# Gated DeltaNet layer on one core: both halves of a group through the block inversion together

## The chip, the cores and the metric

The kernel runs on one core of a Trainium2 chip (eight cores, of which seven stay idle). The metric is the device time of one execution in microseconds. The kernel before was timed three times; the profile is of a fourth execution.

## The reference

One layer of a decoder trunk: adaptive RMSNorm of x (1,024 tokens, width 1,024), a gated DeltaNet mixer, a gated residual and a final RMSNorm. The mixer projects to q and k (8 heads of 128), v and a gate z (16 heads of 128) and two rows of gates, runs a causal convolution of 4 taps with SiLU over q, k and v, and then works in chunks. Cut to what matters:

```python
a_mat = where(strict, einsum('bhncd,bhnsd->bhncs', kb, k) * decay, 0.0)
t_mat = triangular_solve(a_mat + eye, eye, lower=True, unit_diagonal=True)   # an inverse for each chunk and head
u = t_mat @ (v * beta); w = t_mat @ (kb * exp(gc))
def step(state, inp):                    # a scan over the chunks
    v_new = uc - wc @ state
    o = qd @ state + qkc @ v_new
    state = state * gl + kd.T @ v_new
o = rms_norm(o) * silu(z); y = o @ w_out
```

The part that the change touches is `t_mat`, the inverse of a unit lower triangular matrix for each chunk and head.

## The kernel before, in words

The kernel takes chunks of 128 tokens, so a head has 8 chunks, and works on 8 groups of two value heads that share one q and k head. Each group has 16 triangular matrices of 128×128, in two halves (`hf`) of four chunks times two heads. A group passes through these stages.

- `proj_kq` and `values` project the group's q, k and v with three matmuls of 128×512 for each of 8 blocks of width (L448; 24 of them fill one PSUM bank of tag `pj`). Each result goes through `Conv` (ScalarE copies and scales it, L431 and L433, VectorE adds three taps, L435, ScalarE applies SiLU, L436). `turn` in `values` transposes a value tile on TensorE (L628) into a bank of `trans()`, 40 projection matmuls after that tile was done, and VectorE empties the bank (L629).
- `stage_a` makes the matrices `at` and sends their diagonal 32×32 blocks through HBM (D1) to a layout in which VectorE inverts all of them at once by forward substitution (L564 and L566). The result goes to HBM (D2). Then the stage waits D_L0.
- `levels(gi, G, hf)` builds the inverse of one half from the 32×32 inverses, in four steps. Eight DMAs for the group (L585, four a half) fetch the blocks into `TT`; VectorE transposes them into `TE` (L586 to L588). Step 1 multiplies `at` blocks with `TE` (L592 and L594, 16 matmuls of 32×32 in two corners of the array, written to `pa`); ScalarE and VectorE negate the result into `pn` (L598 and L599). Step 2 multiplies `pn` with `TT` (L602 and L603, `px`); VectorE copies the result to `TT` twice and transposes it to `TE` (L606 to L608). Step 3 multiplies 64×64 blocks (L611, `pb`) and ScalarE negates (L614). Step 4 (L617, `pc`) ends with a copy into `TT` (L618). Each of `pa`, `px`, `pb` and `pc` takes a fresh bank from `trans()`: tag `tr`, two banks, shared with L628 and with the transposes of `norms` (L497, L504), the products of `stage_a` (L538) and the matmul of the residual gate (L782).
- `scan` runs the recurrence over the 8 chunks of the group; `TT` of the first half is needed from its first chunk on (L744).

The order of TensorE's instructions is written out by hand: everything runs inside a `manual_schedule` for that engine, and `drive` plays the stages as generators against a model clock. A stage yields a cost (model ns on TensorE) and a delay; it isn't asked again until the delay has passed. While no stage is due, `drive` emits filler, that is projection matmuls, each counted as MM = 216. For group `gi`, one call of `drive` runs `scan(gi)`, `stage_a(gi + 1)` with its levels, and `values(gi + 1)` and `proj_kq(gi + 2)` as filler. For the two groups in `LEV1` (0 and 7) the second half's levels run in the next call, beside the group's own scan. When the stages of a call are done, the filler that is left follows. The order on the other engines, the queue of DMAs on SyncE (SP) among them, is not written out: the Tile framework chooses it and adds the semaphores.

The delays before: D_L1, D_L2 and D_L3 are 1,600, 1,800 and 1,600. The steps of one half, cut to their skeleton:

```python
pa = v8(trans())          # step 1: 16 matmuls, L592 and L594
yield 400, D_L1
px = v8(trans())          # step 2: 16 matmuls, L602 and L603, behind pn (L598, L599)
yield 670, D_L2
pb = v8(trans())          # step 3: 8 matmuls of 64x64, L611, behind L606, L607, L608
yield 430, D_L3
pc = v8(trans())          # step 4: 8 matmuls of 64x64, L617, behind pn2 (L614)
yield 430, D_L3
```

Of the kernel before, what the change touches and what calls it, by code (L numbers as in the profile page):

```python
# [9 lines left out]
F32 = mybir.dt.float32  # L10
# [7 lines left out]
P = 128  # L18
# [12 lines left out]
LEV1 = (0, 7)  # L31
# [6 lines left out]
START, START1 = 8000, 65000  # L38
D_G, D_RG = 6000, 11000
D_N, D_A0, D_A = 3000, 1500, 1000  # L40
D_L0, D_L1, D_L2, D_L3 = 46000, 1600, 1800, 1600
D_R, D_V, D_S = 500, 1100, 700
D_F0, D_F = 8000, 2000

# [2 lines left out]
def gdn_layer(ctx: ExitStack, tc: tile.TileContext, x, c, ada_w, ada_b, norm_g, w_in, conv_w, a_log, dt_bias,  # L47
# [8 lines left out]
    nc = tc.nc  # L56
# [12 lines left out]
    x, c, ada_w, ada_b, norm_g = x[0], c, ada_w[0], ada_b, norm_g  # L69
# [342 lines left out]
    cp = ctx.enter_context(tc.tile_pool(name="cp", bufs=2))  # L412
    TTs = [cp.tile([P, 4, 2, P], F32, name=f"TT{i}", bufs=1) for i in range(3)]
    for t in TTs:
        nc.gpsimd.memset(t, 0.0)
    TE = cp.tile([96, 8, 64], F32, name="TE", bufs=1)
    nc.gpsimd.memset(TE[0:64], 0.0)

    class Conv:

# [32 lines left out]
    def trans():  # L453
        return bank("tr", (P, 4, P))
# [68 lines left out]
    def stage_a(gi, G):  # L523

        kq, ats = G.kq, []
        if not hasattr(G, "bkd"):
            yield from norms(gi, G)
        D1 = dram.tile([16, P, 32], F32, name="D1", tag="D1", bufs=2)
        D2 = dram.tile([16, 4, 16, 2, 32], F32, name="D2", tag="D2", bufs=2)
        yield 0, D_A0  # L530
        for hf in range(NHALF):
            em, brk = G.em[hf], G.brk[hf]

            at = cp.tile([P, 8, P], F32, name="at", tag="at", bufs=2)
            for j in range(4):
                js = slice(j * P, (j + 1) * P)
                pg2 = trans()
                nc.tensor.matmul(pg2[:, 0:2], lhsT=kq[hf][:, 0, js], rhs=kq[hf][:, :, js], start=True, stop=True)  # L538
                for h in range(2):
                    nc.vector.scalar_tensor_tensor(at[:, 2 * j + h], pg2[:, 0], brk[:, j, h:h + 1], em[:, h, j],  # L540
                                                   op0=ALU.mult, op1=ALU.mult)
                nc.vector.tensor_tensor(em[:, :, j], em[:, :, j], pg2[:, 1:2].to_broadcast([P, 2, P]), op=ALU.mult)
                yield 430, D_A
            us = slice(8 * hf, 8 * hf + 8)
            for b in range(4):
                bs = slice(32 * b, 32 * b + 32)
                nc.sync.dma_start(out=D1[us, bs, :].rearrange("u s c -> s u c"), in_=at[bs, :, bs])
            ats.append(at)


        ua = cp.tile([P, 32, 32], F32, name="ua", tag="ua", bufs=1)
        for p in range(2):
            nc.sync.dma_start(out=ua[64 * p:64 * p + 64].rearrange("p s c -> p (s c)"),
                              in_=D1.rearrange("u (b s) c -> (u b) (s c)", b=4))
        tb = cp.tile([P, 16, 32], F32, name="tb", tag="tb", bufs=1)
        tm = cp.tile([P, 136], F32, name="tm", tag="tm", bufs=1)
        tbf = tb.rearrange("p m i -> p (m i)")
        nc.gpsimd.memset(tb, 0.0)
        nc.gpsimd.memset(tbf[0:64, 0:512:34], 1.0)
        nc.gpsimd.memset(tbf[64:128, 1:512:34], 1.0)  # L560
        for j in range(31):
            mm, ln = j // 2 + 1, 31 - j
            tmv = tm[:, :mm * ln].rearrange("p (m l) -> p m l", l=ln)
            nc.vector.tensor_tensor(tmv, tb[:, :mm, j:j + 1].to_broadcast([P, mm, ln]),  # L564
                                    ua[:, j:j + 1, j + 1:].to_broadcast([P, mm, ln]), op=ALU.mult)
            nc.vector.tensor_tensor(tb[:, :mm, j + 1:], tb[:, :mm, j + 1:], tmv, op=ALU.subtract)  # L566
        for p in range(2):
            nc.sync.dma_start(out=D2[:, :, :, p, :].rearrange("u b m i -> (u b) m i"), in_=tb[64 * p:64 * p + 64])

        yield 0, D_L0  # L570
        G.ats, G.D2 = ats, D2
        yield from levels(gi, G, 0)
        if gi not in LEV1:
            yield from levels(gi, G, 1)

    def levels(gi, G, hf):

        TT = TTs[(2 * gi + hf) % 3]
        G.TT.append(TT)
        at = G.ats[hf]  # L580
        tt = TT.rearrange("p n h c -> p (n h) c")
        us = slice(8 * hf, 8 * hf + 8)
        for b in range(4):
            bs = slice(32 * b, 32 * b + 32)
            nc.sync.dma_start(out=tt[bs, :, bs], in_=G.D2[us, b].rearrange("u m p i -> (m p) u i"))  # L585
        nc.vector.transpose(TE[0:32, :, 0:32], tt[0:32, :, 0:32])  # L586
        nc.vector.transpose(TE[32:64, :, 32:64], tt[32:64, :, 32:64])
        nc.vector.transpose(TE[64:96, :, 0:32], tt[64:96, :, 64:96])  # L588
        v8 = lambda t: t.rearrange("p a (b c) -> p (a b) c", c=64)
        pa = v8(trans())  # L590
        for u in range(8):
            nc.tensor.matmul(pa[32:64, u, :32], lhsT=at[0:32, u, 32:64], rhs=TE[0:32, u, 0:32], start=True,  # L592
                             stop=True)
            nc.tensor.matmul(pa[96:128, u, :32], lhsT=at[64:96, u, 96:128], rhs=TE[64:96, u, 0:32], start=True,  # L594
                             stop=True, tile_position=(64, 96))
        yield 400, D_L1
        pn = cp.tile([P, 8, 32], F32, name="pn", tag="pn2", bufs=1)
        nc.scalar.mul(pn[32:64], pa[32:64, :, :32], -1.0)  # L598
        nc.vector.tensor_scalar_mul(pn[96:128], pa[96:128, :, :32], -1.0)  # L599
        px = v8(trans())  # L600
        for u in range(8):
            nc.tensor.matmul(px[0:32, u, :32], lhsT=pn[32:64, u], rhs=tt[32:64, u, 32:64], start=True, stop=True)  # L602
            nc.tensor.matmul(px[64:96, u, :32], lhsT=pn[96:128, u], rhs=tt[96:128, u, 96:128], start=True,  # L603
                             stop=True, tile_position=(96, 64))
        yield 670, D_L2
        nc.vector.tensor_copy(tt[0:32, :, 32:64], px[0:32, :, :32])  # L606
        nc.vector.tensor_copy(tt[64:96, :, 96:128], px[64:96, :, :32])  # L607
        nc.vector.transpose(TE[32:64, :, 0:32], px[0:32, :, :32])  # L608
        pb = v8(trans())
        for u in range(8):  # L610
            nc.tensor.matmul(pb[64:128, u], lhsT=at[0:64, u, 64:128], rhs=TE[0:64, u], start=True, stop=True)  # L611
        yield 430, D_L3
        pn2 = cp.tile([P, 8, 64], F32, name="pn2", tag="pn2", bufs=1)
        nc.scalar.mul(pn2[64:128], pb[64:128], -1.0)  # L614
        pc = v8(trans())
        for u in range(8):
            nc.tensor.matmul(pc[0:64, u], lhsT=pn2[64:128, u], rhs=tt[64:128, u, 64:128], start=True, stop=True)  # L617
        nc.vector.tensor_copy(tt[0:64, :, 64:128], pc[0:64])  # L618
        yield 430, D_L3

    def values(gi, G, more):

# [294 lines left out]
    with tc.manual_schedule(engines={nc.tensor.engine}):  # L917
# [6 lines left out]
        for gi in range(-1, HQ):  # L924
            running.append(gi)
            streams, filler = [], []
            gates = itertools.chain(*zgates[:ZQ[gi + 1]])
            del zgates[:ZQ[gi + 1]]
            if gi >= 0:
                if gi in LEV1:  # L930
                    streams.append(levels(gi, Gs[gi], 1))
                streams.append(scan(gi, Gs[gi]))
            if gi + 1 < HQ:
                if gi < 0:
                    streams.append(gate_steps)
                streams.append(stage_a(gi + 1, Gs[gi + 1]))
                if gi < 0:
                    streams.append(norms(1, Gs[1]))
                more = []
                if gi + 2 < HQ:  # L940
                    Gs[gi + 2].kq = []
                    more = proj_kq(gi + 2, Gs[gi + 2].kq)
                if gi + 2 == HQ:
                    more = itertools.islice(tail, NE)
                v = lambda m: values(gi + 1, Gs[gi + 1], m)
                filler += (more, v(gates)) if gi < 0 else (gates, v(more))
            else:
                filler.append(gates)
            if gi == RG:
                streams.append(residual_gate())  # L950
            drive(streams, filler, start=(D_G, START, START1) if gi < 0 else None, tail=tail if gi >= HQ - 2 else None)
# [8 lines left out]
    for tg in range(2):  # L960
# [7 lines left out]
                    out_product(acc[t][hf], t, gw, ww[hf], kt == EARLY, False)  # L968
        if wlast is None:
            wos += [[cp.tile([P, TH], F32R, name=n, tag=t, bufs=b)  # L970
                        for n, t, b in (("wohi", "sz", 2), ("wolo", ("pn2", "tb")[hf], 1))] for hf in range(1)]
            wlast = [[load_wo(kt, hf, wos[2 * i + hf]) for hf in range(2)] for i, kt in enumerate(last)]
        glast = [load_g(kt, tg, gos[i]) for i, kt in enumerate(last)]

# [50 lines left out]
```

## Time and profile before

| what | value |
|---|---|
| median of 3 runs | 1140.28 us (1137.90 to 1142.37) |
| the profiled execution's own time | 1136.89 us |
| its span, first to last instruction | 1135.2 us |
| busy time of PE, VectorE (DVE), ScalarE (ACT), GpSimd (POOL) | 1054.0, 764.9, 534.5, 454.0 us |
| mean granted TensorE clock | 0.969 |
| DMA | 119.46 MB, mean 105 GB/s |

Times in the profile are counted from the first instruction. PE is TensorE's matmul row. Its matmuls overlap and their ends are modelled, so what one costs in a stream is read from the distance of two starts. An "idle before" in brackets names what the engine waited for. [...]

### The profile page before, as it was taken

How to read it: one execution, taken by the hardware profiler on the slowest of the kernel's cores; microseconds unless marked ns; L12 is line 12 of the kernel's file. 1: busy time of each engine (PE TensorE's matmuls, PEld its weight loads, DVE VectorE, ACT ScalarE, POOL GpSimd, SP SyncE). 2: the span in 40 equal slices, each digit the busy share in tenths (PEclk: the TensorE clock that was granted, in tenths of full speed). 3: DMA queues.
4: the chain of work that ended last, by engine and by line, in shares of the span. 5: the costliest groups of instructions: out<-in, count | busy, mean ns of one | idle time of the engine just before them, and what ended most of it. 6: DMA issues, size and time to landing. Idle time of an engine off the chain costs nothing.

```text
span 1135.2 us, 18160 instructions
## 1 busy us (share of the span) xinstructions
PE 1054.0 (93%) x6195; PEld 847.9 (75%) x6195; DVE 764.9 (67%) x1937; ACT 534.5 (47%) x1414; POOL 454.0 (40%) x535
## 2 busy tenths in 40 slices
PE   7677999989999899989999999999999979999997
PEld 6455787767778678867876887788778858878785
DVE  5968794785579866965687578667756866614515
ACT  5556534444553445345543644364446423634523
POOL 4361213532253225323532353245215433954743
PEclk8888999999999899999999999999999989999999
DMA  9903314342135323421442153115313472346442
GB/s 281 238 19 123 75 57 117 84 126 61 29 100 179 96 54 80 144 56 29 112 121 66 29 149 93 39 45 160 75 29 88 155 222 76 121 144 187 157 121 74
DMA packets 188130, 119.46 MB, mean 105 GB/s; under 512 B 59733, under 2 KB 166534, under 8 KB 187014
## 3 DMA queue, kind: packets, MB, share of 16 engines
q1 hardware_dynamic: 187536, 118.20, 37.0%
q8 instruction: 49, 0.80, 0.3%
q14 instruction: 43, 0.35, 0.1%
q10 hardware_dynamic: 502, 0.10, 0.0%
HBM read 93.03 MB, written 25.24 MB: 104 GB/s over the span
## 4 chain that ended last, share of the span: by engine, by line
PE 37%; DVE 19%; issue 6%; POOL 6%; ACT 5%; DMA 5%; SPq 0%; POOLq 0%; DVEq 0%; ACTq 0%
PE pj L448 16%; DVE tb L566 4%; DVE tm L564 4%; PE pj L826 4%; DVE vT L435 3%; DVE em L486 3%; POOL wolo L123 2%; PE tr L538 2%; PE ks L725 2%; PE ks L756 2%; PE ts L744 1%; PE oq L698 1%; PE oq L751 1%; PE tr L611 1%; PE tr L617 1%
## 5 line engine op out<-in xcount | busy, mean ns | idle before, releaser
L123 POOL TENSOR_TENSOR wlo<-wraw,whi 128x512 fp32r<-128x512 f32 x92 | 124.8, 1365 | 140.6 <-ACT whi L122 106.3
L435 DVE SCALAR_TENSOR_TENSOR vT<-xb,taps,vT 128x512 f32<-128x512 f32 x96 | 84.6, 881 | 25.3 <-ACT vT L433 24.3
L435 DVE SCALAR_TENSOR_TENSOR kq<-xb,taps,kq 128x512 f32<-128x512 f32 x96 | 78.2, 823 | 11.9 <-ACT kq L433 10.0
L122 ACT CAST whi<-wraw 128x512 fp32r<-128x512 f32 x92 | 55.4, 618 | 62.3 <-PE pj L448 58.7
L687 POOL TENSOR_TENSOR oT<-oT,z 128x256 f32<-128x256 f32 x64 | 51.3, 801 | 82.2 <-ACT oT L686 74.9
L564 DVE TENSOR_TENSOR tm<-tb,ua 128x126 f32<-128x126 f32 (+22 forms) x248 | 79.1, 319 | 6.5 <-DMA ua<-D 1.6
L686 ACT ACTIVATE oT<-pot,cols 128x256 f32<-128x256 f32 x64 | 30.4, 474 | 110.4 <-PE pot L684 53.8
L448 PE MATMUL pj<-h1hia,whi 128*128 128x512 f32 x184 | 76.0, 413 | 6.7 <-ACT vT L433 6.7
L566 DVE TENSOR_TENSOR tb<-tb,tm 128x126 f32<-128x126 f32 (+22 forms) x248 | 77.3, 312 | 5.0 <-DVE tm L564 0.2
L448 PE MATMUL pj<-h1lob,whi 128*128 128x512 f32 x184 | 78.8, 428 | 0.0
L448 PE MATMUL pj<-h1hia,wlo 128*128 128x512 f32 x184 | 78.5, 427 | 0.0
L448 PE MATMUL pj<-h1hib,whi 128*128 128x512 f32 x184 | 78.3, 426 | 0.0
L448 PE MATMUL pj<-h0hia,whi 128*128 128x512 f32 x184 | 76.5, 416 | 1.3 <-ACT kq L433 1.3
L448 PE MATMUL pj<-h0lob,whi 128*128 128x512 f32 x184 | 77.7, 422 | 0.0
L448 PE MATMUL pj<-h1hib,wlo 128*128 128x512 f32 x184 | 77.1, 419 | 0.0
L448 PE MATMUL pj<-h1loa,whi 128*128 128x512 f32 x184 | 76.3, 415 | 0.0
L448 PE MATMUL pj<-h0hib,wlo 128*128 128x512 f32 x184 | 76.1, 413 | 0.0
L448 PE MATMUL pj<-h0loa,whi 128*128 128x512 f32 x184 | 75.7, 411 | 0.0
L448 PE MATMUL pj<-h0hia,wlo 128*128 128x512 f32 x184 | 75.5, 410 | 0.0
L428 POOL MEMSET xb<- 128x3 f32 x32 | 3.4, 109 | 179.8 <-DVE kq L435 90.8
L448 PE MATMUL pj<-h0hib,whi 128*128 128x512 f32 x184 | 74.8, 407 | 0.0
L708 POOL TENSOR_TENSOR sso<-sso,neg_half 128x2 f32<-128x2 f32 x64 | 44.6, 697 | 58.4 <-DVE sso L707 57.7
(445 smaller groups left out, 2938.0 us busy)
## 6 DMA issues: line engine op xcount, KB each, us to landing
wraw<-in_gdn_w_in SPq DMA_DIRECT2D x92, 256.0 KB, 2.9
woraw<-in_gdn_w_out SPq DMA_DIRECT2D x54, 256.0 KB, 3.1
wa<-in_ada_w SPq DMA_DIRECT2D x16, 512.0 KB, 6.4
em<-gc_dram SPq DMA_DIRECT2D x8, 1024.0 KB, 5.2
z_dram<-sz SPq DMA_DIRECT2D x32, 256.0 KB, 2.5
z<-z_dram SPq DMA_DIRECT2D x64, 128.0 KB, 2.4
o_dram<-oT SPq DMA_DIRECT2D x64, 128.0 KB, 1.9
gsrc<-o_dram SPq DMA_DIRECT2D x32, 256.0 KB, 3.0
```

The lines of the kernel that those rows point to most:

```text
L122: nc.scalar.copy(hi, raw)
L123: nc.gpsimd.tensor_tensor(lo, raw, hi.bitcast(F32), op=ALU.subtract)
L435: nc.vector.scalar_tensor_tensor(dst, xb[:, j:j + TH], tp[:, j], dst, op0=ALU.mult, op1=ALU.add)
L448: nc.tensor.matmul(ps[:m], lhsT=a[:, k, :m], rhs=b[half][k // 4][:, k % 4], start=(k == 0 and n == 0), stop=(k == KT - 1 and n == 2))
L486: nc.vector.scalar_tensor_tensor(em[:, h, n], em[:, h, n], ngc[:, n, h0 + h:h0 + h + 1], mask, op0=ALU.add, op1=ALU.add)
L538: nc.tensor.matmul(pg2[:, 0:2], lhsT=kq[hf][:, 0, js], rhs=kq[hf][:, :, js], start=True, stop=True)
L564: nc.vector.tensor_tensor(tmv, tb[:, :mm, j:j + 1].to_broadcast([P, mm, ln]), ua[:, j:j + 1, j + 1:].to_broadcast([P, mm, ln]), op=ALU.mult)
L566: nc.vector.tensor_tensor(tb[:, :mm, j + 1:], tb[:, :mm, j + 1:], tmv, op=ALU.subtract)
L686: nc.scalar.mul(oT, pot, normw_c)
L687: nc.gpsimd.tensor_tensor(oT, oT, zs.pop(n), op=ALU.mult)
L708: nc.gpsimd.tensor_tensor(sso, sso, neg_half[:, :2], op=ALU.pow)
L826: nc.tensor.matmul(acc, lhsT=a[:, ts], rhs=b, start=(first and n == 0), stop=(last and n == 2))
```

## The change

`levels` takes a tuple of halves. Groups 1 to 6 call it once with both halves, groups 0 and 7 with one half at a time as before. Within a call each step is done for all its halves before the next yield, with a bank of `trans()` for each half; `TE` gets a second copy and `pn2` a second buffer. The transposes behind step 2 move ahead of the copies. D_L1, D_L2 and D_L3 become 2,600, 2,800 and 2,000, and step 2's model cost for a half 400 instead of 670. The DMA scratch (`dynamic_dma_scratch_size`) is set to 1,024, and the tile of the last stage that reuses tag `pn2` follows its two buffers.

```diff
-D_L0, D_L1, D_L2, D_L3 = 46000, 1600, 1800, 1600
+D_L0, D_L1, D_L2, D_L3 = 46000, 2600, 2800, 2000
...
-    TE = cp.tile([96, 8, 64], F32, name="TE", bufs=1)
-    nc.gpsimd.memset(TE[0:64], 0.0)
+    TEs = [cp.tile([96, 8, 64], F32, name=f"TE{i}", bufs=1) for i in range(2)]
+    for t in TEs:
+        nc.gpsimd.memset(t[0:64], 0.0)
...
-        yield from levels(gi, G, 0)
-        if gi not in LEV1:
-            yield from levels(gi, G, 1)
+        yield from levels(gi, G, (0,) if gi in LEV1 else (0, 1))
...
+        for i, hf in enumerate(hfs):
+            us = slice(8 * hf, 8 * hf + 8)
+            for b in range(4):
+                bs = slice(32 * b, 32 * b + 32)
+                nc.sync.dma_start(out=tt[i][bs, :, bs], in_=G.D2[us, b].rearrange("u m p i -> (m p) u i"))
+            nc.vector.transpose(TE[i][0:32, :, 0:32], tt[i][0:32, :, 0:32])
...
+        pa = [v8(trans()) for _ in every]
+        for i in every:
+            for u in range(8):
+                nc.tensor.matmul(pa[i][32:64, u, :32], lhsT=at[i][0:32, u, 32:64], rhs=TE[i][0:32, u, 0:32], start=True,
+                                 stop=True)
...
+        yield 400 * len(hfs), D_L1
+        pn = [cp.tile([P, 8, 32], F32, name="pn", tag="pn2", bufs=2) for _ in every]
+        for i in every:
+            nc.scalar.mul(pn[i][32:64], pa[i][32:64, :, :32], -1.0)
+            nc.vector.tensor_scalar_mul(pn[i][96:128], pa[i][96:128, :, :32], -1.0)
+        px = [v8(trans()) for _ in every]
...
+        yield 400 * len(hfs), D_L2
+        for i in every:
+            nc.vector.transpose(TE[i][32:64, :, 0:32], px[i][0:32, :, :32])
+        for i in every:
+            nc.vector.tensor_copy(tt[i][0:32, :, 32:64], px[i][0:32, :, :32])
+            nc.vector.tensor_copy(tt[i][64:96, :, 96:128], px[i][64:96, :, :32])
+        pb = [v8(trans()) for _ in every]
...
+        yield 430 * len(hfs), D_L3
+        pn2 = [cp.tile([P, 8, 64], F32, name="pn2", tag="pn2", bufs=2) for _ in every]
+        for i in every:
+            nc.scalar.mul(pn2[i][64:128], pb[i][64:128], -1.0)
+        pc = [v8(trans()) for _ in every]
...
+        yield 430 * len(hfs), D_L3
...
-    nc = bacc.Bacc("TRN2", target_bir_lowering=False, num_devices=1)
+    nc = bacc.Bacc("TRN2", target_bir_lowering=False, num_devices=1, dynamic_dma_scratch_size=1024)
```

## Rows read from the trace of the kernel before

**Rows 1.** Page, busy us (share of the span) and instructions of each engine.

```profile
PE 1054.0 (93%) x6195; PEld 847.9 (75%) x6195; DVE 764.9 (67%) x1937; ACT 534.5 (47%) x1414; POOL 454.0 (40%) x535
```

**Rows 2.** Page, the chain that ended last, share of the span by line.

```profile
PE pj L448 16%; DVE tb L566 4%; DVE tm L564 4%; PE pj L826 4%; DVE vT L435 3%; DVE em L486 3%; POOL wolo L123 2%; PE tr L538 2%; PE ks L725 2%; PE ks L756 2%; PE ts L744 1%; PE oq L698 1%; PE oq L751 1%; PE tr L611 1%; PE tr L617 1%
```

**Rows 3.** Waits of PE in the levels: us in all, times, longest.

```profile
PE tr L602 <- ACT pn L598: 3.9, 5, 0.8
PE tr L603 <- DVE pn L599: 3.8, 6, 0.7
...
PE tr L611 <- DVE TE L608: 0.6, 1, 0.6
```

**Rows 4.** Timeline of PE in the levels of group 4: start, us, what.

```profile
607.59 0.21 PE L592 MATMUL tr<-TE,at 32*32 32x32 f32 x1
...
609.95 0.39 PE L448 MATMUL pj<-h1hia,whi 128*128 128x512 f32 x1
611.13 0.24 PE L602 MATMUL tr<-TT,pn 32*32 32x32 f32 x2 [0.79 <-ACT pn L598]
612.07 0.21 PE L603 MATMUL tr<-TT,pn 32*32 32x32 f32 x1 [0.69 <-DVE pn L599]
...
614.18 0.60 PE L628 MATMUL tr<-ident,vT 128*128 128x128 f32 x4
...
619.24 0.51 PE L448 MATMUL pj<-h0loa,whi 128*128 128x512 f32 x1
...
621.30 0.21 PE L592 MATMUL tr<-TE,at 32*32 32x32 f32 x1
...
621.93 0.50 PE L448 MATMUL pj<-h0hia,whi 128*128 128x512 f32 x1
```

**Rows 5.** Windows: us, busy PE, PEld, DVE, ACT, POOL (count), PEclk, DMA, GB/s.

```profile
378.80:382.20 3.40, 3.40 (x10) 2.62 (x9) 3.33 (x10) 3.37 (x3) 0.81 (x4) 0.50 0.51 114
392.40:395.90 3.50, 3.50 (x10) 2.38 (x8) 3.40 (x10) 0.63 (x1) 0.19 (x1) 0.51 0.21 59
...
505.10:508.50 3.40, 3.40 (x11) 2.54 (x9) 1.99 (x5) 0.63 (x1) 0.10 (x1) 0.50 0.00 0
...
720.10:723.50 3.40, 3.40 (x17) 2.56 (x16) 1.97 (x4) 0.63 (x1) 0.10 (x1) 0.50 0.00 0
```

**Rows 6.** Timeline of VectorE in the levels of group 4, first half.

```profile
608.87 0.68 DVE L629 TENSOR_TENSOR vtok<-tr,rinv 128x512 f32<-128x512 f32 x1
...
611.58 0.43 DVE L599 TENSOR_SCALAR pn<-tr 32x256 f32<-32x256 f32 x1
612.04 1.54 DVE L435 SCALAR_TENSOR_TENSOR kq<-xb,taps,kq 128x512 f32<-128x512 f32 x2
613.61 0.41 DVE L606 COPY TT<-tr 32x256 f32<-32x256 f32 x1
...
614.48 0.44 DVE L608 STREAM_TRANSPOSE TE<-tr 32x256 f32<-32x256 f32 x1
```

**Rows 7.** Timelines around step 1 of group 1 (VectorE) and group 2 (PE, VectorE).

```profile
269.59 0.69 DVE L629 TENSOR_TENSOR vtok<-tr,rinv 128x512 f32<-128x512 f32 x1 [0.51 <-PE tr L628]
...
387.88 0.50 PE L448 MATMUL pj<-h0hib,wlo 128*128 128x512 f32 x1
...
389.81 0.68 DVE L629 TENSOR_TENSOR vtok<-tr,rinv 128x512 f32<-128x512 f32 x1
```

**Rows 8.** Timelines of PE and ScalarE at step 3 of group 7.

```profile
942.39 1.11 PE L611 MATMUL tr<-TE,at 64*64 64x64 f32 x16
...
943.54 0.59 ACT L614 ACTIVATE pn<-tr 64x512 f32<-64x512 f32 x1 [0.77 <-PE tr L611]
```

**Rows 9.** Timeline of POOL behind the prologue; page, first DMA queue (packets, MB, share).

```profile
85.62 0.52 POOL L417 MEMSET TE<- 64x512 f32 x1
...
98.62 0.10 POOL L428 MEMSET xb<- 128x3 f32 x1 [11.54 <-DVE xb L430]
...
q1 hardware_dynamic: 187536, 118.20, 37.0%
```

More of the change, by code (lines that the diff above doesn't have):

```diff
@@ L571, in stage_a @@
         G.ats, G.D2 = ats, D2
-        yield from levels(gi, G, 0)
-        if gi not in LEV1:
-            yield from levels(gi, G, 1)
[L576 to L588, printed above, removed]
-        v8 = lambda t: t.rearrange("p a (b c) -> p (a b) c", c=64)
[L590 to L619, printed above, removed]
@@ new lines, in stage_a, with levels @@
+        yield from levels(gi, G, (0,) if gi in LEV1 else (0, 1))
+    def levels(gi, G, hfs):
+        TT = [TTs[(2 * gi + hf) % 3] for hf in hfs]
+        TE = [TEs[hf] for hf in hfs]
+        at = [G.ats[hf] for hf in hfs]
+        tt = [t.rearrange("p n h c -> p (n h) c") for t in TT]
+        G.TT += TT
+        every = range(len(hfs))
+        for i, hf in enumerate(hfs):
[4 more added lines that the diff above has]
+            nc.vector.transpose(TE[i][0:32, :, 0:32], tt[i][0:32, :, 0:32])
+            nc.vector.transpose(TE[i][32:64, :, 32:64], tt[i][32:64, :, 32:64])
+            nc.vector.transpose(TE[i][64:96, :, 0:32], tt[i][64:96, :, 64:96])
+        v8 = lambda t: t.rearrange("p a (b c) -> p (a b) c", c=64)
+        pa = [v8(trans()) for _ in every]
[3 more added lines that the diff above has]
+                                 stop=True)
+                nc.tensor.matmul(pa[i][96:128, u, :32], lhsT=at[i][64:96, u, 96:128], rhs=TE[i][64:96, u, 0:32],
+                                 start=True, stop=True, tile_position=(64, 96))
+        yield 400 * len(hfs), D_L1
[5 more added lines that the diff above has]
+        for i in every:
+            for u in range(8):
+                nc.tensor.matmul(px[i][0:32, u, :32], lhsT=pn[i][32:64, u], rhs=tt[i][32:64, u, 32:64], start=True,
+                                 stop=True)
+                nc.tensor.matmul(px[i][64:96, u, :32], lhsT=pn[i][96:128, u], rhs=tt[i][96:128, u, 96:128], start=True,
+                                 stop=True, tile_position=(96, 64))
+        yield 400 * len(hfs), D_L2
[5 more added lines that the diff above has]
+        pb = [v8(trans()) for _ in every]
+        for i in every:
+            for u in range(8):
+                nc.tensor.matmul(pb[i][64:128, u], lhsT=at[i][0:64, u, 64:128], rhs=TE[i][0:64, u], start=True,
+                                 stop=True)
+        yield 430 * len(hfs), D_L3
+        pn2 = [cp.tile([P, 8, 64], F32, name="pn2", tag="pn2", bufs=2) for _ in every]
+        for i in every:
+            nc.scalar.mul(pn2[i][64:128], pb[i][64:128], -1.0)
+        pc = [v8(trans()) for _ in every]
+        for i in every:
+            for u in range(8):
+                nc.tensor.matmul(pc[i][0:64, u], lhsT=pn2[i][64:128, u], rhs=tt[i][64:128, u, 64:128], start=True,
+                                 stop=True)
+            nc.vector.tensor_copy(tt[i][0:64, :, 64:128], pc[i][0:64])
+        yield 430 * len(hfs), D_L3
@@ L930, in gdn_layer @@
                 if gi in LEV1:
-                    streams.append(levels(gi, Gs[gi], 1))
+                    streams.append(levels(gi, Gs[gi], (1,)))
                 streams.append(scan(gi, Gs[gi]))
@@ L970, in gdn_layer @@
             wos += [[cp.tile([P, TH], F32R, name=n, tag=t, bufs=b)
-                        for n, t, b in (("wohi", "sz", 2), ("wolo", ("pn2", "tb")[hf], 1))] for hf in range(1)]
+                        for n, t, b in (("wohi", "sz", 2), ("wolo", ("pn2", "tb")[hf], 2))] for hf in range(1)]
             wlast = [[load_wo(kt, hf, wos[2 * i + hf]) for hf in range(2)] for i, kt in enumerate(last)]
```

## Prediction, made before the change was run

> **What bounds the kernel now.** Read first the busy table: TensorE (PE) is busy 93% of the span and no other engine comes near [rows 1]. The chain that ended last agrees: its largest single share is the projection matmuls of L448 [rows 2]. PE runs its instructions in the order in which `drive` emitted them, so time is gained only where PE stands still or pays for a change between kinds of matmul. Next read PE's waits: the block inversion makes PE wait in step 2, five times for ScalarE's `pn` (3.9 us in all) and six times for VectorE's `pn` (3.8 us) [rows 3]. Then the timeline of one steady group shows what a step costs. In group 4 step 1 starts at 607.59; the last projection matmul ahead of step 2 starts at 609.95, step 2 at 611.13 instead of some 0.32 later, and its first L603 at 612.07 instead of 0.05 later [rows 4]. That is 0.86 + 0.89 = 1.75 us of standstill. Groups 3 to 6 repeat this pattern. The second half of each waits nowhere: its steps are only islands in a stream of L448.
>
> An undisturbed step also has a price beside its own matmuls. Eight L448 lie between 619.24 and 621.30; at the 0.233 us at which they otherwise follow each other they would take 1.86, so entering and leaving the stream costs 0.20 us [rows 4].
>
> [...]
>
> **The change, part by part.** Six groups (1 to 6) get both halves in each step; groups 0 and 7 keep single halves and get only the longer delays. Numbers of matmuls, transposes, copies and DMAs stay the same.
>
> *Fewer islands.* Eight steps become four: 4 × 0.20 us, and the 0.03 us by which the first pair of a 32×32 step is slower falls away a few times; I take -0.92 us a group. Bounds: 0 if the islands only grow longer, -1.0.
>
> *Step 2's wait.* With D_L1 at 2,600 instead of 1,600 and MM at 216, 13 L448 instead of 8 stand between step 1 and step 2, some 1.2 us more cover, and the second half of step 1 adds 0.6. In rows, VectorE's `pn` of the first half starts at 611.58, 4.0 us behind the start of step 1 [rows 6]; step 2 now starts at least 4.4 us behind it. So the 1.75 us go: bounds 0 (nothing gained) and -1.75, taken whole.
>
> *What is late next: the two PSUM banks.* All steps, and the transposes of L628, take their bank from `trans()`, two buffers of tag `tr`. Before, a step of one half used one buffer while the other was being emptied. Now step 1 wants both. In group 4 one of them still holds the transposes of L628 that precede the levels; VectorE empties it in L629, which starts at 608.87 and takes 0.68, behind a value convolution [rows 6]. A half's step 1 takes 0.62 us (621.30 to 621.93 [rows 4]), so the second half would start at 608.21 and stands until 609.55: +1.35 us. Bounds: 0 if VectorE's order is made otherwise (nothing below 0, a held bank can't speed PE up), and +2.1 if one 0.75 us tap of L435 goes ahead of L629.
>
> The next place is L628 itself. Before, 8 + 6 = 14 L448 lie between step 1 and L628 at 614.18 [rows 4]; after, 13 of them come before step 2, so one L448 separates step 2 from L628, and both banks then hold `px`. L628 must wait until VectorE has read the first `px` three times: the transposes of both halves (0.44 each, L608) stand first, then two copies (L606, 0.41, and L607, which is like it) [rows 6]. From the end of the first half's matmuls this takes about 0.05 + 0.44, then the second transpose after the second half's matmuls (0.61 to 1.05), then two copies, 0.82: 1.9 us, while PE arrives after 0.9. +1.0 us. Bounds: +0.45 if the copies of the first half overtake the second transpose, +2.5 if the two taps of a key convolution that stand ahead of L606 now (1.54 us, at 612.04) stay ahead [rows 6].
>
> [...]
>
> *Steps 3 and 4.* 2,800 and 2,000 put 10 L448 (2.3 us) behind the transposes and 10 ahead of step 4. ScalarE's L614 takes 0.59 a half; in group 7 it starts 1.15 us behind the start of step 3 [rows 8], so ten L448 cover both halves. 0; bounds 0 and +0.5 where another ScalarE operation stands between.
>
> A steady group: -0.92 - 1.75 + 1.35 + 1.0 = -0.32 us; four of them, -1.3.
>
> *Group 1* has no wait to lose. L629 of the transposes ahead of its levels ends at 270.28 [rows 7], against 270.11 wanted (step 1 starts at 269.49): +0.2; a second L628 falls between step 2 and step 3 and holds a bank for step 3: +0.2. With -0.92: -0.5. *Group 2* loses its waits, 0.8 and 0.4 in the first half, 0.6 at its second L603 and 0.6 at L611 (together 2.4, parts of [rows 3]), and the islands, 0.92. But VectorE is full of the residual gate there: L629 ends at 390.49, and the second half of step 1 wants to start at 387.88 [rows 7]: +2.6; and the gate's matmul L782, also on `tr`, now falls right behind step 2: +1.0. Together +0.3.
>
> *Groups 0 and 7, longer delays without filler.* In both, the filler of that drive ends with the levels: 28 L448 after step 1 of group 0 (8 + 9 + 8 by the delays, and 3 more), 24 L826 for group 7 (9 + 9 by the delays, in units of three, and 6 more). Longer delays draw it forward, and nothing is left ahead of step 4. In group 7 step 3 starts at 942.39 and L614 runs from 943.54 to 944.13 [rows 8]; step 4 then starts 1.8 us after step 3 started, against 1.07 us of matmuls: +0.75 a group, +1.5 for both less one island saved, about +1.45 in all. Bounds 0 and +3.
>
> *The rest.* The second TE memset costs about 0.52 us on POOL as the first did, and POOL then idles 11.5 us before its next wait ends [rows 9]: 0. The loads of both halves are already issued as one train before the levels, so moving four of them up the SP queue passes nothing: 0. The smaller DMA scratch: nearly all packets are on hardware queues [rows 9], no row shows the scratch in use: 0, with no row for either bound, and SP's issue is not on PE's path. The added buffers can only remove waits: 0.
>
> Sum: -1.3 - 0.5 + 0.3 + 1.45 = -0.05 us against the profiled execution's 1136.89, which lies 3.4 us under the median of 1140.28. On the median: 1140 us.
>
> **The rivals.**
> *Faster.* The waits for the banks do not appear, because VectorE's order, which is made anew, puts L629 and the copies earlier. Then the steady groups give -2.67 each, group 2 -3.3, group 1 -0.9: -14.9 + 1.45 = -13.4, and up to four half-clock stretches (-1.7 each) can go too: 1120 to 1134, and with part of the waits kept about 1129. For it: VectorE idles now and then in the levels. Against: L629 stands behind a convolution that is needed sooner.
> *Slower, the banks decide.* The held `tr` buffer is emptied later than I take: L628 waits 2.5 us (the key convolution stays ahead) in groups 3 to 6 and L629 one tap later. That gives +1.5 + 0.75 = +2.25 a group, +9 in all: about 1149. It decides from about +1.4 us a group on. For it: today's order on VectorE [rows 6]. [...]
> *The change doesn't do what it says:* the halves share a step in name, but the second stands in line for its bank, so PE pays inside the step what it paid between steps. That is my forecast's middle, no change.
>
> **How the numbers follow.** About 0.5% (5.7 us) is what a measurement of this kernel can tell from no change. Forecast, waits move rather than go: 0.47, with its own range 1135 to 1146. Faster rival: 0.30. Slower rival: 0.23. The range for 8 in 10 reaches into both, by the bounds of the bank waits (-9.4 us if they vanish in the steady groups, +9 if they grow): 1130 to 1148.
>
> **What would show it.** Right: step 2's waits for `pn` gone; new PE waits in the second half of step 1 (for VectorE L629) and at the transposes of L628 (for the copies of `px`), 1 to 1.4 us each, four times; 14 L448 between step 1 and L628; short waits at step 4 of groups 0 and 7. Wrong: no wait at those places and groups shorter by over 1 us, or a distance between groups that grows by more than 1 us; a change outside the levels, such as VectorE's order around the `em` exponentials, would mean that I looked in the wrong place.

## The result, and the profile after

The change made the kernel slower. Four runs had a median of 1152.97 us (1146.76 to 1157.07) against 1139.09 for the kernel before (four runs); the ratio is 1.012, interval 1.009 to 1.015. The forecast was no change, 1140.0 with a range up to 1148.0, so the time lies outside it. The profiled execution took 1146.76 us, the fastest of the four; its span is 1145.0 against 1135.2.

Line numbers have moved: L448 is L449 now, step 1 is L596 and L598 (were L592, L594), step 2 L608 and L610, step 3 L621, step 4 L630, the transposes of a value tile L642 (L628), their emptying L643 (L629), the gate's matmul L796 (L782), the copies and transposes behind step 2 L614, L616 and L617.

The page of the changed kernel, busy times and the chain by line, answering [rows 1, 2]:

```profile
PE 1044.6 (91%) x6195; PEld 845.4 (74%) x6195; DVE 759.0 (66%) x1937; ACT 536.8 (47%) x1416; POOL 455.8 (40%) x536
...
PE pj L449 15%; DVE tb L567 4%; DVE tm L565 4%; DVE vT L436 4%; PE pj L840 3%; DVE em L487 2%; POOL wolo L123 2%; DMA woraw<-in_gdn_w_out 2%; PE tr L539 2%; PE ts L758 1%; PE ks L739 1%; PE tr L630 1%; PE tr L621 1%; PE oq L712 1%; PE ks L770 1%
```

PE does the same 6,195 matmuls and is busy for a smaller share: it stands still more. Where, say the waits of PE over the whole execution (us in all, times, longest), answering [rows 3]:

```profile
PE tr L596 <- DVE vtok L643: 6.0, 5, 1.5
PE tr L642 <- DVE TT L617: 5.2, 5, 1.2
...
PE tr L796 <- DVE accg L230: 4.8, 1, 4.8
...
PE tr L596 <- DVE TE L589: 3.0, 1, 3.0
...
PE tr L796 <- DVE TT L617: 1.4, 1, 1.4
```

The waits of step 2 for `pn`, 7.7 us in all before, are gone. Two waits for a `tr` bank, five times each, have come in their place, and one wait of 4.8 us at the residual gate. The timeline of PE in group 4 shows the first two, answering [rows 4]:

```profile
619.58 0.21 PE L596 MATMUL tr<-TE,at 32*32 32x32 f32 x1 [1.45 <-DVE vtok L643]
...
626.06 0.63 PE L642 MATMUL tr<-ident,vT 128*128 128x128 f32 x4 [1.01 <-DVE TT L617]
```

And the timeline of VectorE in the same stretch, answering [rows 6]:

```profile
618.84 0.68 DVE L643 TENSOR_TENSOR vtok<-tr,rinv 128x512 f32<-128x512 f32 x1
...
624.16 0.44 DVE L614 STREAM_TRANSPOSE TE<-tr 32x256 f32<-32x256 f32 x1 [0.17 <-PE tr L610]
624.62 0.41 DVE L616 COPY TT<-tr 32x256 f32<-32x256 f32 x1
625.04 0.44 DVE L614 STREAM_TRANSPOSE TE<-tr 32x256 f32<-32x256 f32 x1
625.50 0.42 DVE L617 COPY TT<-tr 32x256 f32<-32x256 f32 x1
```

L643 ends at 619.52 and the second half of step 1 starts at 619.58. The first `px` has had its last reader at 625.92 and L642 starts at 626.06.

To see where the time went, I take the start of each group's first scan matmul (the first row `ts<-vtok` of each group) and its distance in us from the one of the group before. Each distance holds the levels of the group named; that of group 1 holds the second half of group 0 too, and the second half of group 7 falls behind the last distance.

| kernel (profiled execution) | group 1 | 2 | 3 | 4 | 5 | 6 | 7 |
|---|---|---|---|---|---|---|---|
| before | 112.3 | 115.7 | 109.3 | 106.4 | 108.0 | 106.3 | 98.2 |
| changed, first | 113.8 | 121.7 | 111.7 | 105.9 | 106.1 | 106.1 | 98.7 |
| changed, second (`again`) | 114.1 | 122.1 | 112.9 | 109.1 | 109.1 | 109.1 | 98.6 |

In the first execution groups 4 to 6 are a little shorter than before, and most of the loss sits in group 2 and at the start of group 3. In the second, which is nearer to the median, groups 4 to 6 are 3 us longer than in the first, and group 3 is 1.2 us longer. The same program gave both: what differs is the granted clock, 0.973 and 0.962 in the mean, as the next section shows.

### The profile page after: what moved, and what is told of

It reads as the page before. It is cut to its first block, busy times and chain, and to the rows that moved or that the text cites. A ratio compares the mean times of both kernels' runs of the same rounds, so it can differ in the third digit from the quotient of the medians.

```text
span 1145.0 us, 18131 instructions
## 1 busy us (share of the span) xinstructions
PE 1044.6 (91%) x6195; PEld 845.4 (74%) x6195; DVE 759.0 (66%) x1937; ACT 536.8 (47%) x1416; POOL 455.8 (40%) x536
## 4 chain that ended last, share of the span: by engine, by line
PE 33%; DVE 20%; POOL 7%; issue 6%; DMA 6%; ACT 4%; SPq 1%; POOLq 0%; DVEq 0%; ACTq 0%
PE pj L449 15%; DVE tb L567 4%; DVE tm L565 4%; DVE vT L436 4%; PE pj L840 3%; DVE em L487 2%; POOL wolo L123 2%; DMA woraw<-in_gdn_w_out 2%; PE tr L539 2%; PE ts L758 1%; PE ks L739 1%; PE tr L630 1%; PE tr L621 1%; PE oq L712 1%; PE ks L770 1%
## 5 line engine op out<-in xcount | busy, mean ns | idle before, releaser
L123 POOL TENSOR_TENSOR wlo<-wraw,whi 128x512 fp32r<-128x512 f32 x92 | 126.3, 1381 | 134.4 <-ACT whi L122 104.1
L436 DVE SCALAR_TENSOR_TENSOR vT<-xb,taps,vT 128x512 f32<-128x512 f32 x96 | 83.6, 871 | 19.9 <-ACT vT L434 18.7
L436 DVE SCALAR_TENSOR_TENSOR kq<-xb,taps,kq 128x512 f32<-128x512 f32 x96 | 75.4, 791 | 25.2 <-ACT kq L434 23.7
L449 PE MATMUL pj<-h1hia,whi 128*128 128x512 f32 x184 | 77.0, 419 | 6.3 <-ACT vT L434 6.3
L449 PE MATMUL pj<-h0hia,whi 128*128 128x512 f32 x184 | 76.6, 417 | 1.3 <-ACT kq L434 1.3
L449 PE MATMUL pj<-h1hia,wlo 128*128 128x512 f32 x184 | 77.6, 422 | 0.0
L449 PE MATMUL pj<-h0lob,whi 128*128 128x512 f32 x184 | 77.5, 421 | 0.0
L429 POOL MEMSET xb<- 128x3 f32 x32 | 3.3, 110 | 185.8 <-DVE kq L436 104.0
L449 PE MATMUL pj<-h1lob,whi 128*128 128x512 f32 x184 | 77.2, 419 | 0.0
L449 PE MATMUL pj<-h1hib,whi 128*128 128x512 f32 x184 | 76.8, 417 | 0.0
L449 PE MATMUL pj<-h0hia,wlo 128*128 128x512 f32 x184 | 76.1, 413 | 0.0
L449 PE MATMUL pj<-h1loa,whi 128*128 128x512 f32 x184 | 76.0, 413 | 0.0
L449 PE MATMUL pj<-h0hib,wlo 128*128 128x512 f32 x184 | 75.9, 412 | 0.0
L449 PE MATMUL pj<-h1hib,wlo 128*128 128x512 f32 x184 | 75.5, 410 | 0.0
L449 PE MATMUL pj<-h0hib,whi 128*128 128x512 f32 x184 | 75.3, 409 | 0.0
L449 PE MATMUL pj<-h0loa,whi 128*128 128x512 f32 x184 | 75.2, 409 | 0.0
```

The costliest lines, as they stand in the source:

```text
L123: nc.gpsimd.tensor_tensor(lo, raw, hi.bitcast(F32), op=ALU.subtract)
L436: nc.vector.scalar_tensor_tensor(dst, xb[:, j:j + TH], tp[:, j], dst, op0=ALU.mult, op1=ALU.add)
L449: nc.tensor.matmul(ps[:m], lhsT=a[:, k, :m], rhs=b[half][k // 4][:, k % 4], start=(k == 0 and n == 0), stop=(k == KT - 1 and n == 2))
```

## The experiments

Each kernel is timed beside the kernel before on its own chip, and the ratios are to that.

### The changed kernel once more

No edit.

> The changed kernel once more, for a second profiled execution. Theory G (the residual gate): the wait of 4.8 us at the last gate matmul (L796, for VectorE's accg) and the half-clock stretch behind it (6.8 us at 424 us of the first profile, so 3.4 us lost) stand here again, since they follow from the order of instructions. Theory B (the two tr banks): the waits of 1.5 us in step 1 and 1.0 us at L642 stand again in groups 3 to 6. Theory C (the clock): the four runs of the changed kernel had mean clocks of 0.973, 0.967, 0.964 and 0.963 at 1146.8, 1152.2, 1157.1 and 1153.7 us, so their spread is the clock's; a profile above 1150 us must show more half-clock stretches in the levels of groups 3 to 6 than the first one, behind the bank waits. Ratio to the kernel before 1.009 to 1.015.

Measured: 1154.42 us against 1135.91, ratio 1.016 (1.014 to 1.018), just above the range expected. The waits in the levels and at the gate are the same to a tenth. The clock is not. In windows of group 4 (us; busy PE, PEld, DVE, ACT, POOL with counts; PEclk; DMA share; GB/s), the first execution had

```profile
619.50:622.90 3.40, 3.32 (x44) 2.79 (x45) 2.25 (x6) 1.79 (x5) 0.00 (x0) 1.00 0.12 37
626.50:629.90 3.40, 3.40 (x28) 2.67 (x27) 0.99 (x2) 1.47 (x3) 0.80 (x1) 1.00 0.02 5
```

and the second, just behind the wait of step 1 and just behind that of L642, in groups 4 and 5,

```profile
623.20:626.60 3.40, 3.40 (x10) 2.65 (x8) 2.62 (x5) 0.69 (x2) 0.11 (x1) 0.50 0.00 0
630.00:633.40 3.40, 3.40 (x10) 2.68 (x9) 0.99 (x2) 0.09 (x1) 0.00 (x0) 0.50 0.02 5
732.40:735.80 3.40, 3.40 (x10) 2.46 (x8) 2.54 (x5) 0.63 (x1) 0.11 (x1) 0.50 0.00 0
739.20:742.60 3.40, 3.40 (x11) 2.63 (x10) 0.91 (x2) 0.26 (x1) 0.00 (x0) 0.51 0.00 0
```

Two half-clock stretches, 3.4 us each at a granted clock of 0.50, stand in group 4 and two in group 5. Group 6 has two as well (841.6 and 848.5), and in group 3 the 20 us over the levels have a mean of 0.83, as in groups 4 to 6: eight in all. By the granted clock about 1.7 us are lost in each, an estimate, half of 3.4; by the distances of groups 4 to 6, which are 3.0 to 3.2 us longer than in the first execution, it is 1.5 to 1.6. So about 13.6 us go to the clock there by the same estimate, against 3.4 (two stretches) before [rows 5]. The first execution of the changed kernel, with one such stretch in group 3 (513.0, at 0.51) and none in 4 to 6 (1.00 over the levels), was the exception; all four runs of this batch had a mean clock of 0.960 to 0.964. Why the same waits left the clock up in that execution, no run shows.

Not every wait of this length was followed by a low clock. In the second execution PE also waits ahead of the levels of group 4, in the stream of projection matmuls, and the clock stays at 1.00 behind both waits; groups 3, 5 and 6 repeat them:

```profile
605.42 0.50 PE L449 MATMUL pj<-h1hia,whi 128*128 128x512 f32 x1 [1.63 <-ACT vT L434]
...
610.28 0.66 PE L642 MATMUL tr<-ident,vT 128*128 128x128 f32 x4 [0.85 <-ACT vT L437]
```

```profile
603.40:619.40 16.00, 13.52 (x62) 9.95 (x60) 11.16 (x17) 8.80 (x14) 6.49 (x8) 1.00 0.39 79
```

The two waits that are followed by the low clock stand beside the small matmuls of the levels. Whether these matter was not separated.

### A second buffer for the gate's weights

```diff
-LAG, ZB, WGB = 3, 3, 1
+LAG, ZB, WGB = 3, 3, 2
```

> A second buffer for the gate's weight tile (WGB 2), so that VectorE's last products no longer wait for a transfer issued only after the first half was read. The order on TensorE stays. Theory G: the wait at the last L796 falls from 4.8 us to under 1.5 and the half-clock stretch behind it goes, so 5 to 8 us are gained: ratio to the kernel before 1.004 to 1.008. Rival (the banks and the clock alone make the loss): the wait shrinks but the time doesn't move by more than 2 us, ratio 1.010 to 1.014.

Measured: 1147.35 us (1140.21 to 1157.05, ten runs), ratio 1.011 (1.008 to 1.014), 0.005 below the changed kernel beside it. The 7 us of medians lie within the 5 to 8 that the theory of the gate asked. Its ratio was missed and lies in the rival's range, since the expectation started from the first batch's 1.012, and the two intervals overlap. The trace is clearer. Group 2 takes 119.7 us and group 3 107.2, against 121.7 and 111.7 in the changed kernel's first execution, and PE waits for `accg` nowhere. What it was, show the rows of the changed kernel's first execution, PE's first:

```profile
415.78 0.28 PE L796 MATMUL tr<-ones,accg 128*128 128x1 f32 x2
...
425.41 0.56 PE L796 MATMUL tr<-ones,accg 128*128 128x1 f32 x2 [4.80 <-DVE accg L230]
```

VectorE in the same stretch:

```profile
417.90 0.74 DVE L436 SCALAR_TENSOR_TENSOR kq<-xb,taps,kq 128x512 f32<-128x512 f32 x1
418.56 0.60 DVE L228 SCALAR_TENSOR_TENSOR accg<-wag,cols,accg 128x128 f32<-128x128 f32 x2
422.00 2.39 DVE L228 SCALAR_TENSOR_TENSOR accg<-wag,cols,accg 128x128 f32<-128x128 f32 x4 [2.84 <-DMA wag<-in_ada_w]
424.32 0.74 DVE L436 SCALAR_TENSOR_TENSOR kq<-xb,taps,kq 128x512 f32<-128x512 f32 x1
424.98 0.28 DVE L230 TENSOR_TENSOR accg<-accg 128x128 f32<-128x128 f32 x1
```

and SP, which issues the transfer that VectorE waits for:

```profile
419.19 0.37 SPq L792 DMA_DIRECT2D wag<-in_ada_w  x1
```

The gate's last product is a chain: the matmul before it frees `accg`, VectorE makes half the sums, only then is the weight buffer free for the next transfer, and the other half follows. From one matmul to the next it takes 9.6 us here. TensorE's hand-written order had covered it before with filler and with a whole step 4 between the last two gate matmuls (411.48 and 418.10, no wait). With the levels drawn together only 19 projection matmuls, 4.4 us, are left. But the chain has grown as well. In the kernel before, VectorE's part of it was

```profile
412.26 0.61 DVE L228 SCALAR_TENSOR_TENSOR accg<-wag,cols,accg 128x128 f32<-128x128 f32 x2
...
415.79 1.14 DVE L228 SCALAR_TENSOR_TENSOR accg<-wag,cols,accg 128x128 f32<-128x128 f32 x4
416.96 0.29 DVE L230 TENSOR_TENSOR accg<-accg 128x128 f32<-128x128 f32 x1
```

so it ended 5.8 us behind the start of the gate's matmul (417.25), and in the changed kernel 9.5 us behind it (425.26). There three convolution taps (L436) stand among the first half of the sums and one ahead of L230. VectorE's new order, with 3.7 us more, thus makes more of the wait than the lost cover does: PE had work for 6.6 us between the two gate matmuls before, and for 4.8 us here. The clock is low for 6.8 us here, at 0.50, from 1.1 us before the end of the wait:

```profile
424.30:431.10 6.80, 5.44 (x21) 4.92 (x22) 2.86 (x7) 2.80 (x10) 0.00 (x0) 0.50 0.21 57
```

At most 4.8 + 3.4 = 8.2 of the 9.8 us by which the first execution's span grew stand here; the 3.4 is an estimate, half of 6.8. That is where they lie in the trace; what is gained for good when the wait goes is less clear (7 us of medians in this kernel, 0.3% with free banks, below). The wide spread of the ten runs goes with their mean clocks, 0.975 at 1140.2 and 0.960 at 1157.1: the bank waits are still in this kernel.

### Other banks for the second half

```diff
-        pa = [v8(trans()) for _ in every]
+        own = lambda i, tag: v8(trans() if i == 0 else bank(tag, (P, 4, P)))
+        pa = [own(i, "ks") for i in every]
...
+        px = [own(i, "ts") for i in every]
...
+        pb = [own(i, "ks") for i in every]
...
+        pc = [own(i, "ts") for i in every]
```

> The second half of each step takes its bank from the scan's tags ks and ts, which stand idle in the levels, instead of the second tr bank; nothing else changes. Theory B: the waits at step 1 (1.5 us, five groups) and at L642 (1.0 to 1.2 us, five groups) go, 10 to 13 us, and with them the half-clock stretches that some executions have there (1.7 us each): ratio to the kernel before 0.995 to 1.002, with the gate's wait of about 4.8 us still there. Theory G alone: these waits were hidden elsewhere and the ratio stays at 1.008 or above.

Measured: 1129.98 us (1128.28 to 1131.99), ratio 0.995 (0.994 to 0.997): faster than both kernels. Waits of PE in groups 3 to 6:

```profile
PE pj L449 <- ACT vT L434: 6.7, 4, 1.8
PE tr L643 <- ACT vT L437: 3.5, 4, 0.9
PE ts L611 <- DVE pn L605: 2.2, 4, 0.6
```

The waits for a bank are gone, a wait of 0.55 us for the second half's `pn` has come, and groups 4 to 6 take 104.0 to 104.1 us, 2 us less than the first execution of the changed kernel. The levels of groups 3 to 6 have no half-clock stretch: the granted clock is 1.00 from 503 to 523, 608 to 628, 712 to 732 and 816 to 836. The gate's wait of 4.8 us is still there.

### The old delays, and the first of them alone

```diff
-D_L0, D_L1, D_L2, D_L3 = 46000, 2600, 2800, 2000
+D_L0, D_L1, D_L2, D_L3 = 46000, 1600, 1800, 1600
```

> Both halves together, but with the old delays (1600, 1800, 1600). The wait of step 1 for the bank stays at 1.5 us; L642 now comes six projection matmuls behind step 2 instead of one, so its wait of 1.0 us goes; step 2 comes 1.2 us earlier and may wait up to 0.7 us for pn. The gate's matmuls fall at other places. Theory B: the time is that of the changed kernel within 4 us, ratio 1.006 to 1.014. Rival (the longer delays cost the time): ratio 1.000 to 1.004.

Measured: 1138.41 us (1134.12 to 1142.89), ratio 1.002 (1.000 to 1.004). The rival holds: with both halves together the longer delays cost the time. The waits of PE in groups 3 to 6 keep the bank wait of step 1 and lose that of L642:

```profile
PE tr L596 <- DVE vtok L643: 5.8, 4, 1.5
...
PE tr L642 <- DVE TT L617: 0.5, 2, 0.3
```

The mean clocks of the ten runs are 0.966 to 0.974, against 0.960 to 0.964 in the second batch of the changed kernel, with the same wait of 1.45 us at step 1 in groups 3 to 6.

The other kernel puts back D_L1 alone (1600, 2800, 2000).

> Both halves together with only the first delay put back (1600; 2800 and 2000 stay). Step 2 then comes eight projection matmuls behind step 1 and L642 six behind step 2, as with all old delays. Theory L (the first delay decides, because 13 matmuls put L642 right behind step 2): no wait at L642 in groups 3 to 6, fewer half-clock stretches, median within 3 us of the one with all old delays (1138), ratio 1.000 to 1.005. Rival (the other two delays cost the time): ratio 1.010 or more.

Measured: 1139.11 us (1136.61 to 1143.37), ratio 1.002 (1.000 to 1.004), as with all old delays. So it is the first delay: 13 projection matmuls behind step 1 put L642 one matmul behind step 2, while both banks are held; eight put it six behind, and its wait is at most 0.3 us. Not all of the gain need come from there: the gate's last wait, too, is 2.1 us in both kernels instead of 4.8.

### The longer delays without the change

```diff
-D_L0, D_L1, D_L2, D_L3 = 46000, 1600, 1800, 1600
+D_L0, D_L1, D_L2, D_L3 = 46000, 2600, 2800, 2000
```

This is an edit of the kernel before; the halves stay one behind the other.

> The kernel before with the longer delays alone, the halves one behind the other. The waits of step 2 for pn (1.7 us in groups 2 to 6) go; L628 finds a free bank, since a single half leaves one. But two halves then want 92 projection matmuls between their steps where 70 are left, so the last two steps of the second half stand bare and wait some 0.8 us each, and the scan's first matmul for the last copy. Theory: 1.000 to 1.006. Rival (the longer delays themselves cost the time): 1.010 or more.

Measured: 1148.51 us, ratio 1.009 (1.007 to 1.012): between the two bounds, so neither theory had its size. The named mechanism is in the waits of PE in groups 3 to 6, the bare step 4 and a `tr` bank at the start of the next group:

```profile
PE tr L617 <- ACT pn L614: 3.4, 3, 1.1
...
PE tr L504 <- DVE TT L618: 1.3, 2, 1.0
```

What I left out is again the clock: its mean is 0.966 to 0.971 in the four runs, against 0.969 to 0.979 in the thirteen of the kernel before beside them. With one half behind the other the longer delays leave step 4 without filler.

### Idle matmuls in the two bank waits

```diff
+        def warm(n):
+            if len(hfs) == 2 and gi >= 2:
+                spare = bank("ks")
+                for _ in range(n):
+                    nc.tensor.matmul(spare[:, :P], lhsT=ones, rhs=ident, start=True, stop=True)
...
         for i in every:
+            if i == 1:
+                warm(12)
...
+        warm(8)
         yield 400 * len(hfs), D_L2
```

Theory C is that standing still brings the granted clock down, and that the usual execution of the changed kernel pays for it. With the two waits filled it asks for no half-clock stretch behind step 1 and L642 in groups 3 to 6, a mean clock of 0.97 or more in every run, a median of 1143 to 1147 and a ratio of 1.006 to 1.010, with little spread.

> In groups 2 to 6 twelve idle 128x128 matmuls (into a bank of tag ks that nothing reads) stand ahead of the second half of step 1 and eight behind step 2, so that TensorE works through the two bank waits of 1.5 and 1.0 us instead of standing still; the waits themselves stay. [...] Rival (the clock falls because of the small matmuls of the levels, or by chance): mean clocks of 0.960 to 0.975 as before, median 1150 to 1156, ratio 1.013 or more.

Measured: 1149.57 us (1149.26 to 1151.00), ratio 1.011 (1.009 to 1.013). The time missed the expectation because I had sized the filling wrongly. Its rows in group 4 are

```profile
615.75 2.94 PE L599 MATMUL ks<-ident,ones 128*128 128x128 f32 x24
...
623.61 2.05 PE L599 MATMUL ks<-ident,ones 128*128 128x128 f32 x16
```

Each of these fp32 matmuls is two rows of 0.12 us, so the filling lasted 2.9 and 2.0 us, longer than the waits. The clock did as theory C said where it was read: 1.00 behind both waits of group 4 (618.6 to 622.0, 625.7 to 629.0) and from 842 to 846 in group 6, mean clocks of 0.975 to 0.981 in all four runs, and a spread under 2 us. The second kernel has 6 and 4.

> The idle matmuls again, now 6 and 4 instead of 12 and 8: each took 0.24 us and not 0.11, so that they lasted 2.9 and 1.8 us, longer than the waits they were to fill (1.5 and 1.0); now 1.4 and 0.9. Theory C: no half-clock stretch behind step 1 and L642 in groups 3 to 6, distance from group to group 106 us as in the first profile of the changed kernel (108 with the long filling, 109 where the clock fell), mean clock 0.973 or more in nearly all runs, median 1141 to 1146, ratio 1.004 to 1.009. Rival (the long filling kept the clock up only because it added work): stretches come back, mean clocks of 0.960 to 0.968, median above 1148, ratio 1.011 or more.

Measured: 1141.42 us (1140.05 to 1143.56), ratio 1.005 (1.003 to 1.007), mean clocks of 0.974 to 0.976, groups 4 to 6 at 106.0 to 106.1 us. Windows over the levels of groups 3 to 6 in this kernel:

```profile
510.00:530.00 20.00, 19.88 (x224) 16.29 (x225) 10.31 (x19) 7.50 (x14) 2.66 (x3) 1.00 0.11 31
617.00:637.00 20.00, 19.89 (x196) 16.18 (x195) 10.79 (x19) 6.75 (x13) 2.67 (x3) 1.00 0.12 28
725.00:745.00 20.00, 19.88 (x196) 16.20 (x195) 10.69 (x19) 6.28 (x11) 2.76 (x4) 1.00 0.10 27
832.00:852.00 20.00, 19.88 (x196) 16.42 (x195) 9.72 (x17) 6.68 (x11) 2.76 (x4) 1.00 0.10 28
```

and in the second execution of the changed kernel:

```profile
510.00:530.00 20.00, 17.53 (x209) 13.66 (x208) 11.11 (x19) 7.20 (x13) 3.10 (x4) 0.83 0.13 35
619.00:639.00 20.00, 17.53 (x207) 13.49 (x207) 11.21 (x19) 7.21 (x13) 3.19 (x4) 0.83 0.13 36
728.00:748.00 20.00, 17.53 (x206) 13.38 (x205) 11.34 (x19) 7.20 (x13) 3.34 (x4) 0.83 0.14 37
837.00:857.00 20.00, 17.53 (x205) 13.32 (x205) 11.46 (x19) 7.13 (x13) 3.43 (x4) 0.83 0.14 38
```

PE stands still for 2.5 us in 20 there and gets 0.83 of its clock. Filled with matmuls whose results nobody reads, the same waits leave it at 1.00. Work was only added, nothing was taken away, and the kernel became 13 us faster (1154.4 to 1141.4 us, ratios 1.016 and 1.005). So the clock is what the usual execution of the changed kernel pays, and without the standing still at these two places it did not fall.

### Banks and gate together, banks with old delays

`bankwag` has both edits, the banks and WGB 2.

> The second half's banks from ks and ts and the second buffer for the gate's weights together. Theory: the two losses are separate, so the time is that of the kernel with the banks (1130) less the 4.8 us of wait at the gate's last matmul, less 3.4 for the half-clock stretch behind it where it goes: 1122 to 1126, ratio 0.988 to 0.992. Rival (the gate's wait only moves to the next transfer): 1128 to 1131, ratio 0.993 to 0.997.

Measured: 1128.13 us (1126.61 to 1131.81), ratio 0.992 (0.989 to 0.995), the lowest of all, but its interval touches that of the banks alone (0.994 to 0.997) and both profiled spans are 1130 us. The ratio is at the edge of what the theory asked, the median in the rival's range. PE no longer waits for `accg`. Group 2 gains 1.6 us and group 3 0.9, while the prologue's end and the tail lie later in that execution. How much of the gate's 4.8 us is saved for good stays open.

`bankold` has the banks and the delays 1600, 1800, 1600.

> The second half's banks from ks and ts, with the old delays. With free banks nothing holds step 1 or L643, so step 2 starts 3.2 us behind the start of step 1, ahead of both pn tiles, and waits some 0.9 us for the first and as much again for the second, in groups 2 to 6. Theory (the longer delays are right once the banks are free): 4 to 8 us slower than the banks with the longer delays, 1133 to 1138, ratio 0.997 to 1.003. Rival (the delays never helped): 1130 or less, ratio 0.995 or below.

Measured: 1137.75 us (1130.10 to 1143.11), ratio 1.001 (0.998 to 1.004), as the theory said. With free banks the longer delays are worth 0.6%; with two shared banks they cost 1.4% (1.002 against 1.016).

## Why the prediction was wrong

*What held.* At full clock the steady groups came out as worked out. Step 2's waits for `pn` went. Step 1 waits 1.45 us for L643 (1.35 predicted), L642 waits 1.01 for the first `px` (1.0 predicted), one matmul behind step 2. The sum was -0.32 us a group; at full clock group 4 changed by -0.5 and group 6 by -0.2. VectorE's order had the copy of the first half ahead of the second transpose, with the second half's transpose between the two copies, so the price came out alike by another order, which is luck. With other banks both waits go, and groups 4 to 6 gain 2 us.

*The step that failed: the clock taken as a draw.* Before, two of the four groups with the same waits had a half-clock stretch (505.1 and 720.1 [rows 5]) and two kept 1.00 over their levels. I took that for a draw and put no change of it into the sum. The rows were right and the reading was not. Before, one pair of waits lay close together in a group [rows 4]; after, two separate ones lie some 6.5 us apart, and the second execution (mean clock 0.962; seven of the eight runs have 0.960 to 0.967) loses the clock behind both: eight stretches in groups 3 to 6 instead of two, 10 us more by the distances. The runs with idle matmuls show it: groups 3 to 6 together take 13 us less in `warm2` than in the second execution of the changed kernel. The slower rival's time, 1149, came near, but its mechanism, L642 waiting 2.5 us, did not occur. In the second execution the clock is at 0.50 behind the waits of 1.45 and 1.01 us; behind its waits of 1.63 and 0.85 us in the projection matmuls it stayed at 1.00. No run shows the 1.7 us that the faster rival takes off for each half-clock stretch as such: it is half of 3.4, and the distances of groups 4 to 6 gave 1.5 to 1.6.

*The gate.* For group 2 I priced the gate's matmul behind step 2 (1.0, measured 1.4) and step 1's wait (2.6, measured 3.0 + 0.6, the second half's transposes queue behind the gate's sums on VectorE). I didn't follow the gate's next matmuls, and the sum has no term for them. Moving the levels' steps together took cover away from another stage in the same `drive` call, and VectorE's new order put convolution taps among the gate's sums. So the gate's last step lost 4.8 us, and up to 3.4 more by the clock (half of the 6.8 us at 0.50, an estimate). Group 2 was to change by +0.3 and changed by 5.9; group 3, which got most of that low clock, by +2.3.

*Small terms.* Group 1 was -0.5 and became +1.5: its second L642 waits 1.2 us for the copies of `px`, a wait that I had put at step 3 with 0.2. The smaller DMA scratch was not run alone; it is in all kernels with the halves together, the faster ones included. Groups 0 and 7 were +1.45 together. Up to the first scan matmul +0.2 came, and the distance of group 7 grew by 0.6; their second halves lie in group 1's distance and behind the last one, which grew by 1.9 in the first execution and shrank by 0.3 in the second.

*The sum, corrected.* The changed kernel's second span is 18.6 us longer than the one before. The groups' distances give 18.8: 1.8 in group 1, 6.3 in group 2, 10.2 in groups 3 to 6 and 0.5 in group 7; the prologue and the tail take 0.2 back. The prediction had waits at nearly all of these places; what its sum lacked is the clock behind them and the gate's last step.

## What to carry to other kernels

When steps that share a small pool of banks are drawn together, count the other users of that pool between them: here two banks served one half and the transposes beside it, but with two halves PE waited 1.45 and 1.01 us. Behind each of these waits the clock cost 1.5 to 1.6 us more in one execution and in the other nothing in groups 4 to 6, so put a price and a chance on it in the sum instead of nothing, and read the mean clocks of several runs; spare banks (ratio 0.995), or failing that idle matmuls (1.005), were worth 1 to 2% here against 1.016. And a hand-written order is one budget of filler: shortening one stage's delays or steps can uncover the chains of the others in the same call, and the order on VectorE changes with it.

## What the runs showed of the hardware

I had not expected that behind waits of 1.45 and 1.01 us, 6.5 us apart, the granted clock of TensorE is 0.50 for 3.4 us each in eight of eight places in one execution and in one of eight in another execution of the same program. Nor that adding idle work makes the kernel faster: 1141.4 us against 1154.4, with spreads of 3.5 and 3.9 us over the runs. An fp32 matmul of 128x128 that is no transpose shows as two rows of 0.12 us each (24 rows in 2.94 us for twelve of them in `warm`); the 128 transposes of L642 show as 128 rows in the changed kernel.
